# The last gate as seven block products, and the projection of p moved to the start of the kernel

## The chip, the cores and the metric

The kernel runs on one core of a Trainium2 chip. The metric is device time in microseconds (us). Engines are named as in the profile: PE is TensorE's matmul, PEld its weight load, DVE is VectorE, ACT is ScalarE, POOL is GpSimd, SP is SyncE, whose queue issues every DMA of this kernel.

## The reference

One layer of a hybrid encoder block on x (1024 tokens by 1024) and p (1024 tokens by 256), all in float32. The change touches the last two lines and nothing of the rest:

```python
h = rmsnorm(x, attn_norm[i]); proj = h @ w_in[i]          # q, k, v, conv_a, conv_g
...                                                       # attention, convolution, x = x + mix @ w_out[i]
h = rmsnorm(x, ffn_norm[i])
x = x + (jax.nn.silu(h @ w_gate[i]) * (h @ w_up[i])) @ w_down[i]
gate = jax.nn.sigmoid(rmsnorm(x, ple_norm[i]) @ w_ple_gate[i])   # (1024 x 1024) @ (1024 x 1024)
x = x + gate * (p[i] @ w_ple_proj[i])                            # (1024 x 256) @ (256 x 1024)
```

## The kernel before, in words

Every float32 product is made of three matmuls (`mm3`, L77): each operand is split into a high part h in a reduced float32 and a low part l = src - h (`split`, L69: ACT makes h, DVE or POOL makes l), and h·h, h·l and l·h are added in PSUM. A matmul has 128 x 128 stationary and 128 x 512 moving values.

The stages follow one another in the program text; a scheduler orders each engine's instructions by their place in the text and by what it expects to be ready, so that work of a later stage can stand among that of an earlier one. Each engine, and SP's queue, then works strictly in the order it was given.

- **Start** (L211 to L222): for each of 8 token tiles t, SP loads x, ACT squares it and DVE normalises it (`xn`, L115, after POOL's power of -0.5, `n_r`, L107), PE transposes it (L121), ACT and DVE split the result into `hT` and `lT`. Weights `wv` are loaded and split beside it, and the first four tiles of v (`pv`) are made from t = 4 on. Then come the convolution (its products `pg` and `pa` first), q, k, and attention.
- **Gate and up products, then the down product** of the feed-forward part, both already made by seven block products in place of eight (Winograd's form of Strassen's scheme: 2 x 2 blocks, sums of blocks multiplied, results combined). `dprod` (L814) is one of the seven down products: 11 steps of two DMAs into `dr`, a split and 12 matmuls. In the second of them the residual x is loaded back (`x1_load`, L798).
- **Last gate** (L878 to L929): for t = 0 to 7 the normed x is transposed and split into `h3`; two of the steps also load a half of p (`pin`), transpose it and split it (`ple_transpose`, L865). Then for two column halves and 8 token tiles: 24 matmuls into `pgt`, a sigmoid on ACT (`psg`), 6 matmuls into `pj` (p's projection), a multiply and an add of x on DVE (L927, L928), a DMA to the output. The very last tile does `pj` and what follows in two halves of 256 columns.

Of the kernel before, what the change touches and what calls it, by code (L numbers as in the profile page):

```python
# [17 lines left out]
P = 128  # L18
S = 1024
# [23 lines left out]
PLT = (0, 3)  # L43
# [9 lines left out]
def hybrid_block(ctx: ExitStack, tc: tile.TileContext, I, out):  # L53
# [760 lines left out]
    def dprod(name, banks, ai, bsrc, first):  # L814
        for p in range(NPR):
            r = cvy.tile([P, 2, 512], F32, name=f"dr{name}{p}", tag="y", bufs=4)
            dma(r[:, 0, :], ga_d[ai][p])
# [4 lines left out]
            l = dhl.tile([P, 2, 512], F32R, name=f"dl{name}{p}", tag="dhl", bufs=8)
            split(h, l, r)
            for q in range(4):
                a = slice(q * P, (q + 1) * P)
# [34 lines left out]
    w4 = es3.enter_context(sb_pool("w4", side="right"))  # L860
    pl = es3.enter_context(sb_pool("pl", side="right"))
    p_in = I["p"][0, 0].rearrange("(t p) c -> p t c", p=P)
    pT = []

    def ple_transpose(c):  # L865
        pin = rawp.tile([P, NT, P], F32, name=f"pin{c}", tag="raw", bufs=2)
        dma(pin, p_in[:, :, c * P:(c + 1) * P])
        h = cvy.tile([P, S], F32R, name=f"pTh{c}", tag="y", bufs=4)
        l = cvy.tile([P, S], F32R, name=f"pTl{c}", tag="y", bufs=4)
        for half in range(2):  # L870
            tp = tbank(f"ptp{c}{half}")
            for tt in range(4):
                nc.tensor.transpose(tp[:, tt, :], pin[:, 4 * half + tt, :], ident)
            hs = slice(half * 512, (half + 1) * 512)
            split(h[:, hs], l[:, hs], tp.rearrange("p a b -> p (a b)"))
        pT.append((h, l))

# [3 lines left out]
    H3 = [[op_pair(pool, f"h3{k}{i}", "act", 4) for i in range(2)] for k, pool in enumerate((map_, mcp))]  # L881

    def h3(w, half, k):
        return H3[k // 4][half][w][:, k % 4, :]

    wpg = I["w_ple_gate"][0].rearrange("(k p) c -> p k c", p=P)
    wpp = I["w_ple_proj"][0].rearrange("(k p) c -> p k c", p=P)
    gsets = [w_set(rawp, wpl, wpg, ch * 512, f"wpg{ch}", 2)
             for ch, wpl in enumerate(([(w8, 8)] * 4, [(w4, 4), (w4, 4), (w8, 8), (w8, 8)]))]
    for g in range(4):  # L890
        gsets[0][0](g)
    for t in range(NT):
        xn = sp3.tile([P, D], F32, name=f"n3_{t}_xn", tag="xin", bufs=2)
        xnorm(x1[:, t, :], gain3, xn, sp3, f"n3_{t}")
        for k in range(2):
            tsplit(xn[:, k * 512:(k + 1) * 512], H3[k][t // 4], t % 4, f"n3_{t}{k}")
        if t in PLT:
            ple_transpose(len(pT))
    for ch in range(2):
        cs = slice(ch * 512, (ch + 1) * 512)  # L900
        pload, wpj = w_set(rawp, [(pl, 2)], wpp, ch * 512, f"wpp{ch}", 2)
        pload(0)
        gload, ws = gsets[ch]
        if ch == 1:
            for g in range(4):
                gload(g)
        for t in range(NT):
            half, tt = t // 4, t % 4
            a = slice(tt * P, (tt + 1) * P)
            ps = mbank(f"pgt{ch}{t}")  # L910
            for k in range(KT):
                wh, wl = ws(k)
                mm3(ps, h3(0, half, k)[:, a], h3(1, half, k)[:, a], wh, wl, k == 0, k == KT - 1)
            sg = t5.tile([P, 512], F32, name=f"psg{ch}{t}", tag="t512", bufs=4)
            nc.scalar.activation(sg, ps, AF.Sigmoid)  # L915
            parts = 2 if ch * NT + t == 2 * NT - 1 else 1
            for i in range(parts):
                w = 512 // parts
                c0 = slice(i * w, (i + 1) * w)
                c1 = slice(ch * 512 + i * w, ch * 512 + (i + 1) * w)  # L920
                pj = mbank(f"pj{ch}{t}{i}")[:, 0:w]
                for k in range(2):
                    wh, wl = wpj(k)
                    mm3(pj, pT[k][0][:, t * P:(t + 1) * P], pT[k][1][:, t * P:(t + 1) * P], wh[:, c0], wl[:, c0],
                        k == 0, k == 1)
# [3 lines left out]
                dma(out[t * P:(t + 1) * P, c1], o)  # L929
# [43 lines left out]
```

## Time and profile before

| what | value |
|---|---|
| median of 3 runs | 1306.11 us (1303.47 to 1308.98) |
| the profiled execution: its own time | 1309.01 us |
| its span, first to last instruction | 1307.2 us |
| PE busy, share of the span | 1263.3 us, 97% |
| DVE, ACT, POOL busy | 68%, 43%, 29% |
| moved by DMA | 193.17 MB, mean 148 GB/s |
| granted TensorE clock, mean | 0.993 |

The durations used below come from that one execution, whose time is 2.9 us above the median. Matmuls are pipelined: what one costs is the distance between the starts of two, not the length in its row.

### The profile page before, as it was taken

Reading aid. Unit: us, or ns where it says so; the run is one execution under the profiler, and the core shown is the slowest. Engines: PE = TensorE matmul, PEld = TensorE weight load, DVE = VectorE, ACT = ScalarE, POOL = GpSimd, SP = SyncE. Lnnn points to the kernel's source line nnn. Section 1 sums busy time; section 2 is a strip of 40 time slices with the busy share of each in tenths; the row PEclk is TensorE's granted clock in tenths of the full one; section 3 lists DMA queues with packets and bytes.
Section 4 is the critical chain, followed back from the end, with each engine's and each line's share of the span. In section 5 each row is a group of like instructions: output and inputs, shape, how many; then the busy total and the mean of one; then the engine's idle time right before and its main releaser. Section 6 shows DMA issues by size and latency. Waiting matters only on the chain.

```text
span 1307.2 us, 16337 instructions
## 1 busy us (share of the span) xinstructions
PE 1263.3 (97%) x6015; PEld 1032.6 (79%) x6015; DVE 892.0 (68%) x1150; ACT 558.2 (43%) x818; POOL 377.4 (29%) x229
## 2 busy tenths in 40 slices
PE   6999999989989999889999999999999999999998
PEld 5888877858878888668888888888887788888887
DVE  6488999778868867966777666767655555566322
ACT  5465654556667654512322222222234443445110
POOL 4399987746665634710000000000000000000000
PEclk9999999999999999989999999999999999999999
DMA  8521323795463335344544544445439765641111
GB/s 277 171 65 33 119 75 105 174 241 122 114 167 109 106 105 193 114 161 153 169 161 161 169 146 161 145 153 164 168 139 383 235 193 192 195 159 65 49 57 41
DMA packets 156868, 193.17 MB, mean 148 GB/s; under 512 B 10919, under 2 KB 91317, under 8 KB 156788
## 3 DMA queue, kind: packets, MB, share of 16 engines
q1 hardware_dynamic: 156788, 192.13, 46.6%
q8 instruction: 47, 0.77, 0.2%
q14 instruction: 33, 0.27, 0.1%
HBM read 134.88 MB, written 57.21 MB: 147 GB/s over the span
## 4 chain that ended last, share of the span: by engine, by line
PE 79%; DVE 9%; DMA 6%; issue 2%; POOL 2%; ACT 1%; SPq 0%; DVEq 0%; POOLq 0%; ACTq 0%
PE Y L79 4%; PE Y L80 4%; PE Y L81 4%; PE Z L79 3%; PE Z L80 3%; PE Z L81 3%; PE X L81 3%; PE X L79 3%; PE X L80 3%; PE dY L79 2%; PE dY L80 2%; PE dY L81 2%; PE pgt L81 2%; PE pgt L80 2%; PE pgt L79 2%
## 5 line engine op out<-in xcount | busy, mean ns | idle before, releaser
L107 POOL TENSOR_TENSOR n_r<-n_ss,mhalf 128x1 f32<-128x1 f32 x24 | 15.0, 631 | 680.8 <-DVE n_ss L106 680.8
L75 DVE TENSOR_TENSOR dl<-dr,dh 128x1024 fp32r<-128x1024 f32 x77 | 94.1, 1224 | 73.8 <-ACT dh L72 71.1
L72 ACT CAST dh<-dr 128x1024 fp32r<-128x1024 f32 x77 | 80.6, 1049 | 105.5 <-PE dY L81 43.8
L316 POOL TENSOR_TENSOR z<-z,pr 128x1024 f32<-128x1024 f32 x45 | 115.8, 2575 | 3.1 <-ACT pr L315 0.8
L311 DVE SCALAR_TENSOR_TENSOR acc<-u,cw,acc 128x1024 f32<-128x1024 f32 x71 | 91.2, 1285 | 1.5
L530 ACT ACTIVATE e<-s,nm 128x1024 f32<-128x1024 f32 x64 | 71.6, 1119 | 37.0 <-DVE nm L527 30.4
L527 DVE TENSOR_REDUCE nm<-s 128x1 f32<-128x1024 f32 x64 | 77.4, 1219 | 10.0 <-PE s L523 4.9
L539 POOL TENSOR_TENSOR e<-e,e 128x1024 f32<-128x1024 f32 x32 | 77.7, 2429 | 2.4
L315 ACT ACTIVATE pr<-u,cw 128x1024 f32<-128x1024 f32 x45 | 51.0, 1149 | 36.4 <-POOL z L316 35.8
L522 PE MATMUL s<-ka,qa 128*128 128x512 f32 x128 | 57.1, 446 | 2.0 <-ACT e L530 1.9
L538 POOL TENSOR_SCALAR e<-e,cf 128x1024 f32<-128x1024 f32 x32 | 36.6, 1144 | 66.4 <-DVE cf L537 28.0
L927 DVE TENSOR_TENSOR o<-pj,psg 128x512 f32<-128x512 f32 (+1 forms) x17 | 11.2, 659 | 63.8 <-PE pj L81 55.5
L80 PE MATMUL dY<-dl,dh 128*128 128x512 f32 x132 | 51.4, 389 | 0.0
L81 PE MATMUL dY<-dh,dl 128*128 128x512 f32 x132 | 51.4, 389 | 0.0
L523 PE MATMUL s<-kb,qb 80*128 80x512 f32 x128 | 51.2, 400 | 0.0
L79 PE MATMUL dY<-dh 128*128 128x512 f32 x132 | 50.4, 391 | 0.0
L75 DVE TENSOR_TENSOR wtl<-wt,wth 128x512 fp32r<-128x512 f32 x64 | 43.2, 683 | 10.5 <-ACT wth L72 10.0
L72 ACT CAST wth<-wt 128x512 fp32r<-128x512 f32 x64 | 36.8, 587 | 20.0 <-PE wt L544 19.7
L915 ACT ACTIVATE psg<-pgt 128x512 f32<-128x512 f32 x16 | 9.6, 599 | 75.6 <-PE pgt L81 75.6
L755 DVE TENSOR_TENSOR aa<-Z,aa 128x512 f32<-128x512 f32 x22 | 15.2, 689 | 36.8 <-PE Z L81 36.8
L80 PE MATMUL av<-wtl,avh 128*128 128x256 f32 x128 | 39.0, 305 | 0.0
L79 PE MATMUL av<-wth,avh 128*128 128x256 f32 x128 | 37.9, 296 | 0.2 <-ACT wth L72 0.2
(355 smaller groups left out, 3979.9 us busy)
## 6 DMA issues: line engine op xcount, KB each, us to landing
dr<-ga_d SPq DMA_DIRECT2D x77, 256.0 KB, 2.7
wr<-in_w_gate SPq DMA_DIRECT2D x44, 256.0 KB, 3.0
wr<-in_w_up SPq DMA_DIRECT2D x44, 256.0 KB, 3.5
wd<-in_w_down SPq DMA_DIRECT2D x22, 512.0 KB, 3.6
wb_d<-wd SPq DMA_DIRECT2D x44, 256.0 KB, 2.0
ga_d<-h SPq DMA_DIRECT2D x44, 256.0 KB, 2.4
dr<-wb_d SPq DMA_DIRECT2D x44, 256.0 KB, 2.9
dr<-in_w_down SPq DMA_DIRECT2D x33, 256.0 KB, 5.3
```

The lines of the kernel that those rows point to most:

```text
L72: nc.scalar.copy(h, src)
L75: (eng_l or nc.vector).tensor_sub(l, src, f32(h))
L79: nc.tensor.matmul(ps, lh, rh, start=first, stop=False, skip_group_check=more)
L80: nc.tensor.matmul(ps, lh, rl, start=False, stop=False, skip_group_check=more)
L81: nc.tensor.matmul(ps, ll, rh, start=False, stop=last, skip_group_check=more)
L311: nc.vector.scalar_tensor_tensor(acc, u[:, k:k + S], cw[:, j, k:k + 1], acc, ALU.mult, ALU.add)
L316: nc.gpsimd.tensor_add(y2, y2, pr)
L522: nc.tensor.matmul(o, qa[:, m, ts_], ka[:, m, kc * 512:(kc + 1) * 512], start=True, stop=False)
L523: nc.tensor.matmul(o, qb[:, m, ts_], kb[:, m, kc * 512:(kc + 1) * 512], start=False, stop=not diag)
L527: nc.vector.tensor_reduce(nm, sp, AX.X, ALU.max, negate=True)
L530: nc.scalar.activation(e, sp, AF.Exp, bias=nm, accum_out=s)
L539: nc.gpsimd.tensor_add(es[0], es[0], es[1])
```

## The change: what it does

Three things, and the diff below is cut to them.

1. **p's projection is made at the start.** p comes already transposed as an input (`pT`), so that it isn't transposed on the chip. `pj_load` loads p and `w_ple_proj` in quarters, at first ahead of x, and splits them; `pj_tile` makes one of 16 tiles (128 x 512) with 6 matmuls, copies it out of PSUM (DVE and ACT by turns) and stores it to `pj_d` in device memory. Four tiles follow each of the first four norms of x.
2. **The last gate is made by seven products** of 512 x 512 blocks (`gprod`, 48 matmuls each: 4 token tiles, 4 steps, 3 parts). Sums of blocks of the normed x are built on DVE and POOL after the transposes (`fs1`, `f11`, `f12`, `f21`) and split afterwards by `comb_split`. Sums of blocks of `w_ple_gate` are made inside the down product (`gate_comb`): 4 times two loads of 512 KB, four subtractions on DVE, four stores of 256 KB to `tg_d`; `gprod` loads them again.
3. **Each output tile** now loads its projection (`pjl`), and goes through `finish`: sigmoid, multiply, add, store; 12 of the 16 have an add ahead of the sigmoid. The last tile is not halved any more.

```diff
+    def pj_load(nms, i):
+        raws = [rp1.tile([P, 2, 512], F32, name=f"{nm}{i}_raw", tag="raw", bufs=3) for nm in nms]
...
+        for k in range(2):
+            for nm, raw in zip(nms, raws):
+                h, l = pq[nm, i]
+                dma(raw[:, k, :], {"p": pT, "w": wpp}[nm][:, k, i * 512:(i + 1) * 512])
+                split(h[:, k, :], l[:, k, :], raw[:, k, :])
+
+    def pj_tile(i):
...
+        ps = mm_tile(f"pj{i}")
+        for k in range(2):
+            mm3(ps, ph[:, k, a], pl[:, k, a], wh[:, k, :], wl[:, k, :], k == 0, k == 1)
+        pj = nat.tile([P, CW], F32, name=f"pjs{i}", tag="nat", bufs=6)
+        if i % 2:
+            nc.scalar.copy(pj, ps)
+        else:
+            nc.vector.tensor_copy(pj, ps)
+        dma(pj_d[i], pj)
+
+    pj_load("pw", 0)
     for t in range(NT):
         xt = cvy.tile([P, D], F32, name=f"x{t}", tag="y", bufs=4)
         dma(xt, x[t * P:(t + 1) * P, :])
...
+        if t == 0:
+            pj_load("p", 1)
+        if t == 1:
+            pj_load("w", 1)
...
         norm_transpose(xt, gain1, t, hT, lT, p1m, f"n1_{t}", xn)
+        for i in range(4):
+            if t < 4:
+                pj_tile(4 * t + i)
...
+            if name == "62" and p in (1, 3, 5, 7):
+                gate_comb(p // 2)
...
+    def gate_comb(k):
+
+        d0 = rawp.tile([P, D], F32, name=f"wg{k}0", tag="raw", bufs=2)
+        d1 = rawp.tile([P, D], F32, name=f"wg{k}1", tag="raw", bufs=2)
+        for i, d in enumerate((d0, d1)):
+            dma(d, wpg[(4 * i + k) * P:(4 * i + k + 1) * P, :])
+        b11, b12, b21, b22 = d0[:, 0:512], d0[:, 512:D], d1[:, 0:512], d1[:, 512:D]
+        V.tensor_sub(b11, b12, b11)
...
+        for i, b in enumerate((b11, b22, b12, b21)):
+            dma(tg_d[i][k], b)
...
+            if t < 4:
+                h, l = A[("pa11", "pa12")[k]]
+                split(h[:, :, ts_], l[:, :, ts_], tp)
+                nc.scalar.copy((f11, f12)[k][:, :, ts_], tp)
+            elif k == 0:
+                nc.scalar.copy(f21[:, :, ts_], tp)
+            else:
+                V.tensor_add(fs1[:, :, ts_], tp, f21[:, :, ts_])
+                h, l = A["pa22"]
+                split(h[:, :, ts_], l[:, :, ts_], tp)
+        if t >= 4:
+            c11, c12, c21, cs1 = [f[:, :, ts_] for f in (f11, f12, f21, fs1)]
+            nc.gpsimd.tensor_sub(c21, c11, c21)
+            V.tensor_sub(c11, cs1, c11)
+            nc.gpsimd.tensor_sub(c12, c12, c11)
...
+        steps = [(g, q) for g in range(2) for q in q4]
+        if last:
+            steps = [(g, q) for q in q4 for g in range(2)]
+        for g, q in steps:
+            a = slice(q * P, (q + 1) * P)
+            for k in range(2):
+                mm3(banks[q], ah[:, 2 * g + k, a], al[:, 2 * g + k, a], ws[g][0][:, k, :], ws[g][1][:, k, :],
+                    first and g + k == 0, g + k == 2, not first)
...
-                mm3(ps, h3(0, half, k)[:, a], h3(1, half, k)[:, a], wh, wl, k == 0, k == KT - 1)
...
-                o = t5.tile([P, w], F32, name=f"o{ch}{t}{i}", tag="t512", bufs=4)
-                nc.vector.tensor_mul(o, pj, sg[:, c0])
-                nc.vector.tensor_add(o, o, x1[:, t, c1])
...
+        pj = pl.tile([P, 512], F32, name=f"pjl{ch}{t}", tag="pj", bufs=4)
+        dma(pj, pj_d[ch * NT + t])
+        nc.scalar.activation(o, src, AF.Sigmoid)
+        V.tensor_mul(o, pj, o)
+        V.tensor_add(o, o, x1[:, t, cs])
+        dma(out[t * P:(t + 1) * P, cs], o)
...
+    gprod("11", GX, "pa11", gblk(0, 0), True)
...
+    comb_split("ps1", fs1)
+    gprod("12", GX, "pa12", gblk(1, 0), False)
+    comb_split("ps2", f11)
+    for q in q4:
+        finish(otile(q, 0), GX[q], q, 0)
...
+    gprod("51", GZ, "ps1", gcmb(0), True)
...
+    gprod("44", GY, "pa22", gcmb(3), False, True)
+    for q in q4:
+        o = otile(4 + q, 0)
+        V.tensor_add(o, GY[q], e1[q // 2][:, q % 2, :])
+        finish(o, o, 4 + q, 0)
```

How the order moves at three places.

PE at its first instructions, before: it begins with the transposes of the first normed tile of x (`n1_0_tp`), then v's first tile.

```order
L121 MATMUL n1_0_tp0_150<-ident_70,xn0_143 128x128 x4
L121 MATMUL n1_0_tp1_157<-ident_70,xn0_143 128x128 x4
L79 MATMUL pv0_274<-wv0_h_139,hT00_125 128x512
L80 MATMUL pv0_274<-wv0_l_140,hT00_125 128x512
L81 MATMUL pv0_274<-wv0_h_139,lT00_129 128x512
```

PE with the change, where the same transposes now stand (rows 19 to 28 of its list, after four tiles of the projection, `pj0` to `pj3`; `p0`, `p1` and `w0` are halves of p and of its weight).

```order
L79 MATMUL pj1_211<-w0_l_148,p0_h_145 128x512
L80 MATMUL pj1_211<-w0_h_147,p0_l_146 128x512
L79 MATMUL pj2_221<-w0_l_148,p0_h_145 128x512
L80 MATMUL pj2_221<-w0_h_147,p0_l_146 128x512
L79 MATMUL pj3_231<-w0_l_148,p0_h_145 128x512
L80 MATMUL pj3_231<-w0_h_147,p0_l_146 128x512
L121 MATMUL n1_0_tp0_187<-ident_86,xn0_180 128x128 x4
L121 MATMUL n1_0_tp1_194<-ident_86,xn0_180 128x128 x4
L78 MATMUL pj4_279<-w0_h_147,p1_h_166 128x512
L79 MATMUL pj4_279<-w0_l_148,p1_h_166 128x512
```

24 matmuls of the projection stand ahead of the first transpose, and all 96 ahead of v's first matmul; from the convolution's first tile up to the last of the gate and up products, PE's order is the same but for some twenty rows in attention.

SP's queue at its start, with the change (from its third DMA on; two of the same kind stand ahead).

```order
L223 DMA p0_raw_143<-in_pT 128x512
L223 DMA w0_raw_144<-in_w_ple_proj 128x512
L243 DMA x0_161<-in_x 128x1024
L245 DMA ident_86<-in_c_ident 128x128
L246 DMA gain1_134<-in_attn_norm 128x1024
L223 DMA p1_raw_165<-in_pT 128x512 x2
L243 DMA x1_241<-in_x 128x1024
L127 DMA wv0_raw_174<-in_w_in 128x2x512
L243 DMA x2_319<-in_x 128x1024
L223 DMA w1_raw_243<-in_w_ple_proj 128x512 x2
```

Before, x's first tile was the first DMA and `wv0` the fourth; now four DMAs of 256 KB stand ahead of x.

DVE in the last gate with the change, at the end of product "12" (`gX`) and the start of "51" (`gZ`), whose operand is `ps1`; `ps2` is that of "62", after it.

```order
L949 TENSOR_TENSOR fs1_10495<-n3_71_10673,f21_10494 128x4x128
L1002 TENSOR_TENSOR o01_10841<-pjl01_10842,o01_10841 128x512
L1002 TENSOR_TENSOR o02_10848<-pjl02_10849,o02_10848 128x512
L1003 TENSOR_TENSOR o01_10841<-o01_10841,x2_8890 128x512
L74 TENSOR_TENSOR ps2l_10825<-f11_10492,ps2h_10824 128x4x128
L74 TENSOR_TENSOR pa22l_10491<-n3_71_10673,pa22h_10490 128x4x128
L1003 TENSOR_TENSOR o02_10848<-o02_10848,x2_8890 128x512
L955 TENSOR_TENSOR f11_10492<-fs1_10495,f11_10492 128x4x128
L74 TENSOR_TENSOR ps1l_10755<-fs1_10495,ps1h_10754 128x4x128
L74 TENSOR_TENSOR ps2l_10825<-f11_10492,ps2h_10824 128x4x128 x2
```

None of these stood there before. The first nine lead from the last transposed tile of x (`n3_71`) to the last quarter of `ps1l`, which product "51" multiplies, and one of the nine (`ps2l`) waits for product "12" to end, since `ps2` lies in the buffer of `pa12`.

## Rows read from the trace of the kernel before

**Rows 1.** The page: busy time of the engines, and the chain's shares by engine

```profile
PE 1263.3 (97%) x6015; PEld 1032.6 (79%) x6015; DVE 892.0 (68%) x1150; ACT 558.2 (43%) x818; POOL 377.4 (29%) x229
PE 79%; DVE 9%; DMA 6%; issue 2%; POOL 2%; ACT 1%; SPq 0%; DVEq 0%; POOLq 0%; ACTq 0%
```

**Rows 2.** Stretches of the span: busy us (and instructions) by engine

```profile
core 0: us, PE busy (x) PEld busy (x) DVE busy (x) ACT busy (x) POOL busy (x), PEclk, DMA share, GB/s
0.00:10.00 10.00, 1.41 (x7) 1.42 (x8) 2.10 (x4) 3.74 (x5) 1.10 (x12) 1.00 0.74 277
10.00:20.00 10.00, 7.36 (x29) 4.85 (x28) 9.01 (x10) 7.88 (x14) 3.44 (x3) 1.00 0.86 298
20.00:30.00 10.00, 10.00 (x44) 8.12 (x42) 8.68 (x9) 6.76 (x10) 6.46 (x5) 0.83 0.95 283
...
160.00:180.00 20.00, 18.64 (x84) 14.89 (x83) 19.93 (x17) 11.76 (x15) 19.55 (x9) 1.00 0.31 93
980.00:1000.00 20.00, 20.00 (x90) 16.54 (x89) 11.26 (x10) 8.52 (x10) 0.00 (x0) 1.00 1.06 395
1000.00:1010.00 10.00, 8.92 (x38) 6.77 (x37) 6.59 (x7) 5.31 (x7) 0.00 (x0) 1.00 1.04 355
...
1070.00:1080.00 10.00, 10.00 (x46) 8.29 (x45) 5.26 (x5) 3.40 (x4) 0.00 (x0) 1.00 0.77 243
...
1230.00:1240.00 10.00, 10.00 (x45) 8.21 (x44) 1.39 (x2) 1.20 (x2) 0.00 (x0) 1.00 0.07 26
```

**Rows 3.** Timeline of PE, start: start us, length us, instruction, idle before

```profile
8.59 1.97 PE L121 MATMUL n_tp<-ident,xn 128*128 128x128 f32 x8 [8.59 <-DVE xn L115]
...
19.67 0.66 PE L121 MATMUL n_tp<-ident,xn 128*128 128x128 f32 x4 [2.59 <-DVE lT L75]
...
43.23 0.39 PE L79 MATMUL pg<-hT,wg_h 128*128 128x512 f32 x1
```

**Rows 4.** Timeline of the end, PE and DVE

```profile
1289.22 0.39 PE L79 MATMUL pgt<-wpg_h,h301h 128*128 128x512 f32 x1
...
1296.18 0.39 PE L79 MATMUL pgt<-wpg_h,h301h 128*128 128x512 f32 x1
...
1303.04 0.28 PE L81 MATMUL pj<-wpp_h,pTl 128*128 128x256 f32 x1
...
1303.96 0.43 DVE L928 TENSOR_TENSOR o<-o,x 128x256 f32<-128x256 f32 x1
```

**Rows 5.** Tiles `pgt` and `pj`: instructions, ns min/median/max, first and last start

```profile
L79 PE MATMUL pgt<-wpg_h,h300h x32: 390/396/483, 1186.8 to 1270.4; 128*128 128x512 f32 x32
L79 PE MATMUL pj<-wpp_h,pTh x34: 278/397/399, 1192.4 to 1302.8; 128*128 128x512 f32 x30, 128*128 128x256 f32 x4
```

**Rows 6.** The chain in order of time, start of the kernel: a group of four transposes

```profile
33.23 0.44 PE n_tp L121 x4
```

**Rows 7.** Timeline of ACT, DVE and POOL, start

```profile
4.37 1.06 ACT L113 ACTIVATE xn<-x 128x1024 f32<-128x1024 f32 x1 [2.37 <-DMA x<-in_x]
15.62 3.40 DVE L115 SCALAR_TENSOR_TENSOR xn<-x,n_r,gain 128x1024 f32<-128x1024 f32 x1 [0.66 <-POOL n_r L107]
37.13 1.29 DVE L115 SCALAR_TENSOR_TENSOR xn<-x,n_r,gain 128x1024 f32<-128x1024 f32 x1
15.55 2.38 POOL L75 TENSOR_TENSOR wv_l<-wv_raw,wv_h 128x1024 fp32r<-128x1024 f32 x1
```

**Rows 8.** Waits from 960 to 1040 us: total us, times, longest

```profile
ACT dh L72 <- DMA dr<-in_w_down: 21.5, 16, 6.0
```

**Rows 9.** Timeline of DVE in the last gate, two instructions back to back

```profile
1203.47 0.68 DVE L75 TENSOR_TENSOR h301l<-n,h301h 128x512 fp32r<-128x512 f32 x1
1204.08 0.68 DVE L927 TENSOR_TENSOR o<-pj,psg 128x512 f32<-128x512 f32 x1
```

**Rows 10.** The page's groups: a split of 1024 columns on DVE (busy us, mean ns)

```profile
L75 DVE TENSOR_TENSOR dl<-dr,dh 128x1024 fp32r<-128x1024 f32 x77 | 94.1, 1224 | 73.8 <-ACT dh L72 71.1
```

**Rows 11.** Tile `n_xn`: a subtraction of 512 columns on POOL

```profile
L661 POOL TENSOR_TENSOR n_xn<-n_xn,n_xn x4: 1270/1295/1302, 511.3 to 534.7; 128x512 f32<-128x512 f32 x4
```

More of the change, by code (lines that the diff above doesn't have):

```diff
@@ L42 @@
 HNT = (0, 3)
-PLT = (0, 3)
 NVL = 2
@@ L97, in hybrid_block @@
     part_d = dram.tile([S, D], F32, name="part_d")
+    pj_d = [dram.tile([P, 512], F32, name=f"pj_d{i}") for i in range(2 * NT)]
     bias_d = dram.tile([(NH + 1) * NB, S], F32R, name="bias_d")
@@ L594, in hybrid_block @@
     ga_d = [[dram.tile([P, 512], F32, name=f"ga_d{i}_{p}") for p in range(NPR)] for i in range(7)]
+    tg_d = [[dram.tile([P, 512], F32, name=f"tg_d{i}_{k}") for k in range(4)] for i in range(4)]
     wb_d = [[dram.tile([P, 512], F32, name=f"wb_d{i}_{p}") for p in range(NPR)] for i in range(4)]
@@ L857, in hybrid_block, with pair, block @@
     es6.close()
-    w4 = es3.enter_context(sb_pool("w4", side="right"))
+    ap = es3.enter_context(sb_pool("ap", side="right"))
     pl = es3.enter_context(sb_pool("pl", side="right"))
[L862 to L876, printed above, removed]
     gain3 = sp3.tile([P, D], F32, name="gain3", tag="gain", bufs=1)
     dma(gain3, I["ple_norm"].to_broadcast([P, D]))
[L881 to L891, printed above, removed]
+    def pair(name, pool=None):
+        return op_pair(pool or map_, name, "act" if pool is None else "a22", 4 if pool is None else 2)
+    def block(name):
+        return mcp.tile([P, 4, 512], F32, name=name, tag="act", bufs=4)
+    A = {n: pair(n) for n in ("pa11", "pa12")}
+    A["pa22"] = pair("pa22", ap)
+    f11, f12, f21, fs1 = block("f11"), block("f12"), block("f21"), block("fs1")
     for t in range(NT):
@@ L894, in hybrid_block @@
         xnorm(x1[:, t, :], gain3, xn, sp3, f"n3_{t}")
+        ts_ = slice(t % 4 * P, (t % 4 + 1) * P)
         for k in range(2):
[L896 to L899, printed above, removed]
[L900 to L929 removed]
@@ new lines, in gcmb, with gprod @@
+    def gcmb(i):
+        return lambda g: [tg_d[i][2 * g + k] for k in range(2)]
+    def gprod(name, banks, a, bsrc, first, last=False):
+        ah, al = A[a]
+        ws = []
+        for g in range(2):
+            r = cvy.tile([P, 2, 512], F32, name=f"gr{name}{g}", tag="y", bufs=4)
+            src = bsrc(g)
+            if isinstance(src, list):
+                for k in range(2):
+                    dma(r[:, k, :], src[k])
+            else:
+                dma(r, src)
+            h = w8.tile([P, 2, 512], F32R, name=f"gh{name}{g}", tag="whl", bufs=8)
+            l = w8.tile([P, 2, 512], F32R, name=f"gl{name}{g}", tag="whl", bufs=8)
+            split(h, l, r)
+            ws.append((h, l))
+        steps = [(g, q) for g in range(2) for q in q4]
[3 more added lines that the diff above has]
+            a = slice(q * P, (q + 1) * P)
+            for k in range(2):
+                mm3(banks[q], ah[:, 2 * g + k, a], al[:, 2 * g + k, a], ws[g][0][:, k, :], ws[g][1][:, k, :],
+                    first and g + k == 0, g + k == 2, not first)
@@ new lines, in finish, with otile @@
+    def finish(o, src, t, ch):
+        cs = slice(ch * 512, (ch + 1) * 512)
+        pj = pl.tile([P, 512], F32, name=f"pjl{ch}{t}", tag="pj", bufs=4)
[4 more added lines that the diff above has]
+        dma(out[t * P:(t + 1) * P, cs], o)
+    def otile(t, ch):
+        return t5.tile([P, 512], F32, name=f"o{ch}{t}", tag="t512", bufs=4)
+    GX = [bank(f"gX{q}", n=q) for q in q4]
@@ new lines, in hybrid_block @@
+    gprod("11", GX, "pa11", gblk(0, 0), True)
+    e1 = [rawp.tile([P, 2, 512], F32, name=f"ge{i}", tag="raw", bufs=2) for i in range(2)]
+    for q in q4:
+        nc.scalar.copy(e1[q // 2][:, q % 2, :], GX[q])
+    comb_split("ps1", fs1)
+    gprod("12", GX, "pa12", gblk(1, 0), False)
+    comb_split("ps2", f11)
+    for q in q4:
+        finish(otile(q, 0), GX[q], q, 0)
+    GZ = [bank(f"gZ{q}", n=4 + q) for q in q4]
+    gprod("51", GZ, "ps1", gcmb(0), True)
+    z5 = block("gz5")
+    for q in q4:
+        V.tensor_add(z5[:, q, :], GZ[q], e1[q // 2][:, q % 2, :])
@@ new lines, in hybrid_block @@
+    comb_split("ps4", f12)
+    GY = [bank(f"gY{q}", n=q) for q in q4]
+    gprod("62", GY, "ps2", gcmb(1), True)
+    aa = block("gaa")
+    for q in q4:
+        V.tensor_add(aa[:, q, :], GY[q], e1[q // 2][:, q % 2, :])
+    comb_split("ps3", f21)
+    gprod("34", GZ, "ps4", gblk(1, 1), False)
+    for q in q4:
+        o = otile(q, 1)
+        V.tensor_add(o, GZ[q], aa[:, q, :])
+        finish(o, o, q, 1)
+    gprod("73", GY, "ps3", gcmb(2), False)
+    for q in q4:
+        o = otile(4 + q, 1)
+        V.tensor_add(o, GY[q], z5[:, q, :])
+        finish(o, o, 4 + q, 1)
```

36 lines of the change are left out of this document (32 added, 4 removed).

## Prediction

> **What bounds the kernel now.** I read the page first: PE is busy for 97% of the span and makes 79% of the chain that ended last [rows 1]. So I took the stretches next, to see where PE is not full. In the last gate it is full to the last tenth, with DVE at 1.4 us of 10 and DMA at 7% [rows 2]: there, each matmul taken away ends the kernel one matmul earlier, as long as the rest follows. At the start PE is not full: it does nothing until the first tile of x is loaded and normed, at 8.59 us, and waits another 2.59 us at 19.67 [rows 3]. Around 980 to 1010 us, in the first down products, DMA is (share 1.04 to 1.06) and PE loses about 1 us in 10 [rows 2]. From 160 to 180 us DVE is full and PE loses 1.4 us [rows 2]; this work keeps its order, so it moves with the start and costs neither more nor less.
>
> The price of a matmul is read from the end, where two tiles' first matmuls stand 6.96 us apart with 30 matmuls between: 0.232 us each [rows 4].
>
> **The change, part by part.**
>
> *The gate's products.* Before: 12 groups of `pgt` matmuls, 32 in each, make 384 [rows 5]. Seven products of 48 are 336. 48 x 0.232 = **-11.1 us**, all on the path, since PE has no gap there.
>
> *The projection leaves the end.* Three groups of 30 whole and 4 half matmuls are worth 96 whole ones [rows 5]: 96 x 0.232 = **-22.3 us**.
>
> *The transposes of p* were four groups of four at 0.44 us [rows 6]: **-1.8 us**. The 16 groups of x stay.
>
> *The last tile's tail.* Before, DVE ended at 1303.96 + 0.43 = 1304.4 us, 1.2 us after the last matmul's end near 1303.2, because the tile was halved [rows 4]. Now add, sigmoid, multiply and add follow the last matmul, each 512 wide and 0.6 to 0.7 us [rows 9]: about 2.8 us, and a store of 256 KB in place of 128. **+1.8 us**; its ends are 1.4 (no gaps) and 2.5.
>
> *The projection at the start.* 96 matmuls more are 22.3 us of PE. What covers them: x's first tile, the first DMA of the queue, was there at 4.37 us [rows 7], and the first quarters of p and of its weight are together as large, so they can be there at about 4.4; with ACT's half of a split (0.6 us) PE can start at 5.0, not 8.59: -3.6. The wait of 2.59 us can be filled: -2.6. After that wait the granted clock was 0.83 on average from 20 to 30 us [rows 2]: about 3.4 us of these ran at the lower level, 1.2 in place of 2.4 GHz, and lost 1.7; without the wait ahead of it I take back 1.5: -1.5. That leaves 14.6 us. Against it: DVE was busy 9.0 and 8.7 us of 10 from 10 to 30 us [rows 2], and gets 8 splits and 8 copies of 512 columns, about 0.61 us each back to back [rows 9], 10 us in all; in its order they stand between the norms, and some of PE's 96 matmuls will wait for a copy to free a bank. I put 2 us on that: **+16.6 us**. The ends: 13 us where DVE never holds PE, and 24 us where nothing is covered (22.3) and x, behind 1 MB of p and w, comes 2 us later. The loads themselves (2 MB) and the stores (4 MB) ride at 280 to 300 GB/s already moving [rows 2]; the weights of v and of the convolution, queued behind the stores on SP, are now needed some 16 us later too, so I cost that at nothing; without that cover each 256 KB store is about 0.9 us of queue.
>
> *The blocks of the gate's weight in the down product.* 4 MB are loaded and 4 MB stored, while 3 MB (gate weights and p) are not loaded there any more: 5 MB more. In 980 to 1000 us DMA moved 395 GB/s and was full [rows 2], and ACT waited 21.5 us in 16 times for the down product's operands [rows 8]. In SP's order as much new traffic stands before the end of that jam as the old weights and p had there, some 2.5 MB each; the rest falls later, where DMA has a quarter free (0.77 busy from 1070 to 1080) [rows 2]. DVE's 16 subtractions, 0.61 us each, are 10 us beside 7 x 11 x 12 = 924 matmuls, over 200 us of PE. I take **+1 us**; the ends are 0 and 12.8 (5 MB at 395 GB/s, nothing hidden).
>
> *New waits in the gate.* DVE now has, from the last down product on: 83 instructions of 512 columns at 0.61 us [rows 9], 10 weight splits at 1.22 [rows 10] and four norms at 1.3 [rows 7]: 68 us, beside 336 x 0.232 + 11 groups of transposes x 0.44 = 83 us of PE. The tightest place is the last quarter of `ps1`: the last tile of x is transposed about 24 us after the down product ends, product "12" ends at about 27, and `ps1l` is the ninth DVE instruction after these transposes: about 31 us, while PE wants that quarter 32 matmuls into "51", at about 34.5. I take **+1 us**; ends 0 and 20 (below).
>
> Row: POOL subtracts 512 columns in 1.3 us [rows 11], and DVE's norm of 1.29 us took 3.40 while POOL split a weight beside it [rows 7]. The Trainium skill says the same of the cause (GPSIMD Engine Reference, Specifications): GpSimd's SBUF interfaces are shared with VectorE, with contention for DVE instructions that have two SBUF inputs. It speaks against this change: the 8 new POOL subtractions, 10.3 us, would be added to DVE's 68 us in the gate, 78 of 83; the sum would still be as above but for the slack of `ps1`, and about 2 us higher.
>
> **Sum:** -11.1 - 22.3 - 1.8 + 1.8 + 16.6 + 1 + 1 = **-14.8 us**. The profiled execution (1309.0) would be 1294.2; the median shown is 2.9 lower, so 1306.1 - 14.8 = **1291.3 us**.
>
> **The rivals.**
>
> *The start is covered better.* DVE keeps up and PE starts dense: +13 at the start, nothing in the down product and the gate: 1306.1 - 35.2 + 1.8 + 13 = 1285.7. For it: 8.6 and 2.6 us of idle PE. Against it: DVE's 9 of 10.
>
> *The start isn't covered.* The loads of p push x back, the copies of the projection push the norms back on DVE, PE waits between them and falls to the lower clock after each wait: 24 us at the start, 1299.7 with 2 us elsewhere. For it: the one wait of 2.59 us before, and DVE. Against it: PE has 24 matmuls ahead of the first norm, six groups of them to bridge the others.
>
> *The jam in the down product grows.* A store of `tg_d` waits on SP for a DVE subtraction, which waits for a load in the jam, and the operands queue behind: half to all of 12.8 us: 1298 to 1303. For it: the queue is strict and full at 1.05. Against it: four operand tiles (`dr`) and four split ones (`dh`, `dl`) can be ahead of PE.
>
> *The gate becomes DVE's, slower than before.* A split of a sum can only start when the product that read its buffer has ended. If the splits of a product run after the end of the one before it, not beside it, then five products each wait for four splits and a part of the weights on DVE, 4 x 0.61 + 2 x 1.22 = 4.9 us, 24 us in all, and each wait would let the clock fall: 1291.3 + 24 = 1315. It decides when a product needs what was freed only one product ago. Against it: `ps1` is read by "51", one product after "11" freed its buffer, and so on: each has a whole product (11 us) for 5 us of DVE. For it: DVE's 68 to 78 us of 83, in strict order.
>
> *It doesn't do what it says.* If p's loads landed so late that PE still began with x, the start would cost its full 22.3, 1297; the order puts 24 matmuls of the projection first, and x's landing at 4.4 us speaks against loads so late; its chance is part of the uncovered start's.
>
> **How the numbers follow.** Forecast (1287 to 1296) 0.58; better covered start (1285 to 1287) 0.12; uncovered start, with the projection that changes nothing there, 0.15 (1296 to 1301); jam 0.09 (1298 to 1303); DVE-bound gate 0.06 (1310 and over). About 0.5% (6.5 us) is what a measurement of this kernel can tell from no change; below 1299.6 lie the first two, 0.12 of the third and 0.04 of the jam: 0.86 faster. The rest of these two, 0.08, is the same, and the last case, 0.06, slower. The range of 8 in 10 runs from 1284 to 1300: from just under the better start to the end of the uncovered one.
>
> **What would show it.** In the profile after: first matmul of PE at about 5 us and the first of the convolution's products (`pg`), at 43.23 before [rows 3], at about 58 to 62, all transposes of x done; from the last down matmul to the last gate matmul about 84 us, where it was 118; the last matmul followed by 2.8 us of ACT and DVE; in 980 to 1020 us no PE wait over 2 us; DVE near 8 of 10 in the gate with PE still full. I am wrong if `pg` starts after 66 us, if PE shows waits on `ps` splits or on `tg_d` loads of several us, or if the gate's matmuls stand further apart than 0.232 us.

## The result and the profile after

The changed kernel takes **1290.52 us** (median of 4 runs, 1288.63 to 1292.45), the kernel before 1306.21 in the same rounds (4 runs, 1303.47 to 1308.98): a ratio of 0.9871, 95% interval 0.9848 to 0.9893. Timed again later, it took 1292.07 us, ratio 0.9882 (0.9865 to 0.9899). The forecast was 1291.3, faster.

The profiled execution took 1289.18 us (span 1287.4), a second one had a span of 1291.9; the one of before had 1307.2. The table cuts these spans at matmuls that all kernels have: the first `pk` (the projection of k, behind the convolution's products), the first transpose of `tt`, the last `X`, the first and last of the down product, the last matmul of the program. From the last `X` to the first down matmul it is 22.3 us in all of them.

| stretch, us | before | changed | changed, again |
|---|---|---|---|
| start to the first `pk` | 156.2 | 170.4 | 170.2 |
| `pk` to `tt` (projections of q and k, attention) | 362.9 | 360.4 | 365.2 |
| `tt` to the last `X` (gate and up products) | 429.3 | 431.7 | 431.6 |
| down product | 214.2 | 213.4 | 213.4 |
| last down matmul to the last matmul (gate) | 118.1 | 82.9 | 82.9 |
| last matmul's start to the end of the span | 4.2 | 6.3 | 6.3 |

So the pair of profiles shows -19.8, and the second one -15.3: the two executions of one program differ by 4.8 in the attention alone. The stretches that the change touches agree within 0.3 us.

The page, as in [rows 1]:

```profile
PE 1249.3 (97%) x5945; PEld 1021.1 (79%) x5945; DVE 937.5 (73%) x1220; ACT 583.0 (45%) x862; POOL 394.4 (31%) x237
PE 81%; DVE 7%; DMA 6%; issue 2%; POOL 2%; ACT 1%; SPq 1%; DVEq 0%; POOLq 0%; ACTq 0%
```

PE has 14 us less, DVE 45 more. The stretches of the changed kernel, columns as in [rows 2], with the whole gate as the last:

```profile
core 0: us, PE busy (x) PEld busy (x) DVE busy (x) ACT busy (x) POOL busy (x), PEclk, DMA share, GB/s
10.00:20.00 10.00, 10.00 (x54) 8.23 (x53) 8.90 (x14) 8.77 (x16) 1.23 (x2) 1.00 1.03 402
20.00:30.00 10.00, 10.00 (x53) 8.18 (x53) 10.00 (x16) 8.27 (x17) 2.84 (x5) 1.00 1.05 408
...
1230.00:1240.00 10.00, 10.00 (x45) 8.11 (x44) 10.00 (x15) 5.74 (x9) 5.31 (x2) 1.00 0.57 178
...
1198.20:1281.50 83.30, 83.27 (x382) 67.80 (x380) 72.89 (x100) 42.39 (x68) 19.46 (x12) 1.00 0.43 139
```

At the start PE is full from 10 us on, with the granted clock at 1.00, where it was 0.83 from 20 to 30 us, and DMA moves 400 GB/s. In the gate PE is as full as before, and DVE, at 1.4 of 10 before, has 72.9 us of 83.3 and is busy throughout from 1230 to 1240. The start on PE, as in [rows 3]:

```profile
4.83 2.07 PE L78 MATMUL pj<-w_h,p_h 128*128 128x512 f32 x4 [4.83 <-ACT w_h L71]
12.18 1.04 PE L121 MATMUL n_tp<-ident,xn 128*128 128x128 f32 x8
...
33.12 1.25 PE L121 MATMUL n_tp<-ident,xn 128*128 128x128 f32 x8 [0.49 <-DVE lT L74]
...
59.44 0.39 PE L78 MATMUL pg<-hT,wg_h 128*128 128x512 f32 x1
```

The first transposes of x come 3.6 us later than before, behind 24 matmuls of the projection, and up to `pk` the only wait after 4.83 is 0.49 us. The end, as in [rows 4] (DVE and ACT behind the last matmul):

```profile
1281.07 0.40 PE L80 MATMUL gY<-gh,pa22l 128*128 128x512 f32 x1
1281.51 0.69 DVE L1044 TENSOR_TENSOR o<-gY,ge 128x512 f32<-128x512 f32 x1
...
1282.23 0.63 ACT L1001 ACTIVATE o<-o 128x512 f32<-128x512 f32 x1 [2.17 <-DVE o L1044]
1282.89 0.69 DVE L1002 TENSOR_TENSOR o<-pjl,o 128x512 f32<-128x512 f32 x1 [0.69 <-ACT o L1001]
1283.62 0.69 DVE L1003 TENSOR_TENSOR o<-o,x 128x512 f32<-128x512 f32 x1
```

Add, sigmoid, multiply, add: 2.8 us in a chain.

### The profile page after: what moved, and what is told of

It reads as the page before. It is cut to its first block, busy times and chain, and to the rows that moved or that the text cites. A ratio compares the mean times of both kernels' runs of the same rounds, so it can differ in the third digit from the quotient of the medians.

```text
span 1287.4 us, 16537 instructions
## 1 busy us (share of the span) xinstructions
PE 1249.3 (97%) x5945; PEld 1021.1 (79%) x5945; DVE 937.5 (73%) x1220; ACT 583.0 (45%) x862; POOL 394.4 (31%) x237
## 4 chain that ended last, share of the span: by engine, by line
PE 81%; DVE 7%; DMA 6%; issue 2%; POOL 2%; ACT 1%; SPq 1%; DVEq 0%; POOLq 0%; ACTq 0%
PE Y L78 5%; PE Y L79 5%; PE Y L80 5%; PE Z L79 3%; PE Z L78 3%; PE Z L80 3%; PE X L80 3%; PE X L78 3%; PE X L79 3%; PE dY L78 2%; PE dY L79 2%; PE dY L80 2%; PE s L562 2%; DVE acc L351 2%; PE s L563 2%
## 5 line engine op out<-in xcount | busy, mean ns | idle before, releaser
L107 POOL TENSOR_TENSOR n_r<-n_ss,mhalf 128x1 f32<-128x1 f32 x24 | 14.7, 617 | 670.1 <-DVE n_ss L106 661.6
L80 PE MATMUL X<-B11h,a11l 128*128 128x512 f32 x88 | 33.5, 401 | 6.5 <-DVE a11l L74 6.5
L584 PE MATMUL wt<-ident,e 128*128 128x128 f32 x256 | 37.5, 273 | 0.3 <-DVE wtl L74 0.2
```

What stands on the lines that cost most here:

```text
L80: nc.tensor.matmul(ps, ll, rh, start=False, stop=last, skip_group_check=more)
```

## The experiments

All ratios are to the kernel before in the same rounds.

**0. The changed kernel again** (`changed_again`).

> The changed kernel as it is, timed in the same rounds as the three below. Theory: as in its first runs, 1290.5, ratio 0.987. Its profile shows which stages move from one execution to the next: the start (`pk` at 170.4), the down product (213.4 us from its first to its last matmul) and the gate (82.9 us from the last down matmul to the last one) within 0.5 us, the attention and the first product behind it by 1 to 3 us.

Measured: as told above. The touched stretches repeat within 0.3 us, which makes them the finer measure below; the attention moves by more than was said.

**1. The projection moved alone** (`proj_moved_alone`). The kernel before, with the start of the change and this in its gate:

```diff
-                pj = mbank(f"pj{ch}{t}{i}")[:, 0:w]
-                for k in range(2):
-                    ...
-                nc.vector.tensor_mul(o, pj, sg[:, c0])
+                nc.vector.tensor_mul(o, pjl[:, c0], sg[:, c0])
```

> The kernel before with p's projection alone moved to the start; the gate keeps its 384 matmuls, its last tile is halved as before. Theory (idle time of PE at the start pays for part of it): the end loses 96 x 0.232 = 22.3 us of matmuls and 1.8 of transposes, the start gains the 14.3 us by which the first matmul of `pk` stands later in the changed kernel, so 9.8 us less than before, about 1296.5 (ratio 0.9925), with `pk` first near 170.5. Rival (the start isn't covered, the whole gain is the gate's): 22.3 to 24 at the start, ratio 0.998 to 1.000.

Measured: 1302.45, ratio 0.9955 (0.9939 to 0.9970). By stretches: first `pk` 170.7 (+14.5), gate 93.6 (-24.5), both as the theory has it; but +1.1 behind the last matmul (the sigmoid used to run beside the projection's matmuls, and now stands in the tail) and +3.8 from `tt` to the last `X`, which the edit doesn't touch. The theory of the start holds; the sum of 9.8 was too good by these two.

**2. No projection** (`no_projection`). `pj_load` and `pj_tile` and their calls are taken out of the changed kernel, and in `finish` a block of x stands in for the projection, so that the output leaves it out:

```diff
-        dma(pj, pj_d[ch * NT + t])
+        dma(pj, x[t * P:(t + 1) * P, cs])
```

> The changed kernel without any of the projection: p and its weight are not loaded, the 96 matmuls, their copies and stores are not made, and the last multiply takes a block of x of the same size in place of the projection. Theory: the start goes back to that of the kernel before (first matmul near 8.6 us, first of `pk` near 156), so about 14 us less than the changed kernel: 1276.5, ratio 0.977. Rival 1, the projection costs its full price or more there: 22 to 24 us less, 1267. Rival 2, it is hidden whole: no difference, 1290.5.

Measured: 1275.61, ratio 0.9752 (0.9724 to 0.9779); first `pk` at 155.7. The whole projection costs 14.7 us at the start, neither its full 22.3 nor nothing.

**3. The projection behind the norms** (`projection_after_norms`). In the changed kernel, the calls in the loop over x are taken out, and behind the loop stands

```diff
+    pj_load("pw", 0)
+    pj_load("p", 1)
+    pj_load("w", 1)
+    for i in range(2 * NT):
+        pj_tile(i)
     es0.close()
```

> The changed kernel with the loads, matmuls, copies and stores of the projection issued behind the loop of the norms and v's products, in place of among them. Theory: the saving at the start is idle time that the projection's matmuls fill, so here PE begins with x again near 8.6 us, the 96 matmuls cost 22.3 us in full, and the kernel takes about 8 us more than the changed one: 1298.5, ratio 0.994. Rival: the place doesn't matter, 1290.5, ratio 0.988.

Measured: 1303.18, ratio 0.9969 (0.9952 to 0.9986): 12 us slower than the changed kernel, first `pk` at 185.2, +29.0 to before and not +22.3. PE's waits up to 185 us:

```profile
PE n_tp L121 <- DVE xn L115: 9.1, 1, 9.1
PE n_tp L121 <- DVE lT L74: 2.6, 1, 2.6
PE pj L78 <- ACT pjs L235: 2.2, 1, 2.2
PE pa L78 <- ACT wa_h L71: 1.7, 1, 1.7
PE pa L80 <- POOL wa_l L74: 0.4, 1, 0.4
```

The first two are those of the kernel before, unfilled. The next three, 4.3 us, are new. ACT's order makes them:

```profile
67.27 1.04 ACT L71 CAST wg_h<-wg_raw 128x1024 fp32r<-128x1024 f32 x1 [5.40 <-DMA wg_raw<-in_w_in]
68.22 1.07 ACT L235 COPY pjs<-pj 128x512 f32<-128x512 f32 x2
71.79 0.59 ACT L235 COPY pjs<-pj 128x512 f32<-128x512 f32 x1 [2.51 <-issue]
72.28 1.05 ACT L71 CAST wa_h<-wa_raw 128x1024 fp32r<-128x1024 f32 x1
```

The copies `pjs`, which free PE's banks, stand behind a split of the convolution's weights that waits 5.40 us for its load, and the split `wa_h` stands behind the last copy. SP issued that load at 62.41, when POOL had freed its buffer, not when a store let it through. The granted clock is also low a second time, 0.91 on average from 60 to 80 us, which is 1.8 us more. The place of the 96 matmuls decides their price.

**4. No sums of weight blocks** (`no_block_sums`). `gate_comb` and its call are left out, and the four `gcmb(i)` become `gblk(...)`: four products take raw blocks of the weight in place of sums.

> The changed kernel without the sums of the gate's weight blocks in the down product: they are not loaded, summed or stored (8 MB of traffic and 16 subtractions on DVE less), and the four products that want sums take raw blocks. Theory: this traffic rides beside matmuls; the down product had a wait of 1.0 us with it and 1.7 before, so within 1.5 us of the changed kernel, 1289 to 1291, ratio 0.987. Rival (the jam): half to all of 12.8 us less, 1278 to 1284.

Measured: 1290.05, ratio 0.9859 (0.9830 to 0.9888); down product 212.0 us, where the kernels with the sums have 212.7 to 213.8. They cost 0.7 to 1.8 us there; no jam.

**5. POOL's subtractions on DVE** (`pool_subs_on_dve`).

```diff
-            nc.gpsimd.tensor_sub(c21, c11, c21)
+            V.tensor_sub(c21, c11, c21)
             V.tensor_sub(c11, cs1, c11)
-            nc.gpsimd.tensor_sub(c12, c12, c11)
+            V.tensor_sub(c12, c12, c11)
```

> The changed kernel with the eight subtractions of POOL in the gate made by DVE. In the changed kernel six of DVE's instructions of 512 columns that run beside one of them take 1.0 to 1.8 us in place of 0.61, about 5.8 us more in all. Theory (the two engines hold each other up): these 5.8 us go and 8 x 0.61 = 4.9 come, so DVE is as full as before, the last split of `ps1` ends about 35 to 36 us after the down product, and the time stays within 1 us, 1290.5. Rival (what lengthens them is something else): DVE has 4.9 us more ahead of the last split of `ps1`, which had 0.8 us to spare; PE waits about 4 us in the product 51: 1294.5.

Measured: 1290.37, ratio 0.9871 (0.9854 to 0.9887); the gate 82.9 us, no wait of PE in it, and the last split of `ps1` ends 36.0 us after the down product in both. The subtractions in the changed kernel (tile `f`: ns min/median/max):

```profile
L949 DVE TENSOR_TENSOR fs<-n,f x4: 678/682/694, 1209.5 to 1227.1; 128x512 f32<-128x512 f32 x4
L954 POOL TENSOR_TENSOR f<-f,f x4: 1296/1488/1748, 1210.3 to 1228.3; 128x512 f32<-128x512 f32 x4
L955 DVE TENSOR_TENSOR f<-fs,f x4: 675/1196/1815, 1212.1 to 1233.0; 128x512 f32<-128x512 f32 x4
L956 POOL TENSOR_TENSOR f<-f,f x4: 1293/2240/5233, 1214.0 to 1233.7; 128x512 f32<-128x512 f32 x4
```

and with the edit:

```profile
L954 DVE TENSOR_TENSOR f<-f,f x4: 682/686/694, 1209.3 to 1230.8; 128x512 f32<-128x512 f32 x4
L955 DVE TENSOR_TENSOR f<-fs,f x4: 681/684/685, 1211.7 to 1234.5; 128x512 f32<-128x512 f32 x4
L956 DVE TENSOR_TENSOR f<-f,f x4: 683/687/693, 1214.2 to 1235.2; 128x512 f32<-128x512 f32 x4
```

With both inputs in SBUF, an instruction on either engine is lengthened by one on the other, DVE's from 0.68 to 1.8 us, POOL's from 1.3 to 5.2; alone on DVE all are 0.69 at most. Eight subtractions handed to POOL freed no time on DVE: in the gate's 83.3 us it is busy for 72.9 us in the changed kernel and for 72.3 with the edit. `fs<-n,f`, which reads `n` from PSUM, was never lengthened.

**6. More work on DVE in the gate** (`dve_plus_8`).

```diff
-                V.tensor_add(fs1[:, :, ts_], tp, f21[:, :, ts_])
+                for _ in range(3):
+                    V.tensor_add(fs1[:, :, ts_], tp, f21[:, :, ts_])
```

> The changed kernel with eight additions of 512 columns more on DVE in the gate (each of the four sums of the lower row's transposes is made three times, with the same result). Theory (DVE is the nearest limit there, the last split of `ps1` ends 0.8 us before PE wants it): 8 x 0.61 = 4.9 us more ahead of it, so PE waits 3 to 4 us in the product 51 and the kernel takes 3 to 4 us more: 1294, ratio 0.990. Rival (by the prediction's sum, 68 us of DVE beside 83 of PE, there is room): 1290.5, no wait of PE over 1 us.

Measured: 1294.94, ratio 0.9907 (0.9892 to 0.9922); the gate 86.6 us, +3.7. PE's waits there:

```profile
PE gY L80 <- DVE ps2l L74: 2.5, 2, 2.1
PE gY L79 <- DVE gl L74: 0.3, 1, 0.3
```

The size is the theory's; the place is one product later, since the planner (the scheduler that orders each engine's instructions) put matmuls of the product 62 ahead of those of 51 that would have waited.

**7. All copies on DVE** (`copies_on_dve`): in `pj_tile`, `nc.vector.tensor_copy(pj, ps)` for every tile.

> The changed kernel with all 16 copies of the projection's results out of their banks on DVE, in place of 8 on DVE and 8 on ACT. Theory (DVE, full from 20 to 30 us, is about to hold PE at the start, as the prediction's 2 us for it say): 8 x 0.61 = 4.9 us more on it, `pk` 2 to 5 us later than 170.4, time 1293 to 1295. Rival (there is room, since PE has matmuls of the projection and of v to go on with): `pk` within 0.5 us of 170.4, 1290.5.

Measured: first `pk` at 172.9, +2.5, as the theory has it, yet 1289.31 us, ratio 0.9859 (0.9843 to 0.9875), no slower. The stretch from `tt` to the last `X` was 429.1, not 431.7. This, and the 3.8 us of run 1, led to that stretch. DVE there, in the changed kernel (second pair of hidden blocks):

```profile
578.08 1.23 DVE L752 TENSOR_TENSOR s<-wr,wr 128x1024 f32<-128x1024 f32 x1 [6.14 <-DMA wr<-in_w_up]
...
581.67 0.69 DVE L786 TENSOR_TENSOR g<-X,g 128x512 f32<-128x512 f32 x1
585.75 1.22 DVE L761 TENSOR_TENSOR s<-wr,s 128x1024 f32<-128x1024 f32 x1 [3.40 <-DMA wr<-in_w_up]
586.90 1.22 DVE L74 TENSOR_TENSOR a11l<-wr,a11h 128x1024 fp32r<-128x1024 f32 x1
588.09 0.69 DVE L818 TENSOR_TENSOR wd<-wd 128x512 f32<-128x512 f32 x1
588.70 0.68 DVE L792 TENSOR_TENSOR bb<-Y,e 128x512 f32<-128x512 f32 x1
```

Both idle times are for loads. At 585.75 it is that of `a12`, for the sum `s4` (L761), and behind it stands `a11l`, for which PE waits 6.5 us (8.7 in the second profile); two rows on, `bb` (it combines this pair's products and frees PE's banks) stands behind `wd` (block sums of the down weights, for the next stage). In the kernels of before and of runs 2 and 7 the planner has it the other way at both places (`a11l`, `s4`, `bb`, `wd`); PE waits 4.2, 1.7 and 2.1 us for `a11l`. There it also waits for `bb`, 1.5, 3.1 and 2.4 us, which it doesn't in the changed kernel.

**8. `s4` off DVE's queue** (`s4_on_pool`).

```diff
-        V.tensor_sub(s4, a12, s2)
+        (nc.gpsimd if p == 1 else V).tensor_sub(s4, a12, s2)
```

> The changed kernel with one subtraction moved: `s4` of the second pair of hidden blocks (`s4 = a12 - s2`), which stands ahead of the split `a11l` on DVE in the changed kernel and behind it in the kernel before, is made by POOL. Theory: DVE's queue is held there by the load of `a12`, with `a11l` (its data there 10 us earlier) behind it, and PE waits for `a11l`, 6.5 to 8.7 us in the changed kernel's executions, 4.2 in the kernel before; without it the wait falls to 4 us or less, the stretch from the first transpose of `tt` to the last product of X from 431.6 us to about 429, and the time by 2 to 3 us, ratio 0.985 to 0.986. Rival (the loads are what is late, whichever instruction is first): the stretch stays at 431.6.

Measured: 1292.90, ratio 0.9879 (0.9858 to 0.9900), stretch 432.7. The theory fell:

```profile
PE Y L78 <- DVE bb L792: 4.6, 1, 4.6
PE X L80 <- DVE a11l L74: 1.8, 1, 1.8
```

Of 6.5 us for `a11l` 1.8 are left, but `wd`, still ahead of `bb`, now stands for its own load, 5.2 us, and PE waits for `bb`. The wait moved on by one instruction, because loads are late for both.

**9. Three edits together** (`s4_pool_subs_halves`): runs 8 and 5, and the last tile in halves:

```diff
+        for i in range(2):
+            c = slice(i * 256, (i + 1) * 256)
+            V.tensor_add(o[:, c], GY[q][:, c], e1[1][:, 1, c])
+            nc.scalar.activation(o[:, c], o[:, c], AF.Sigmoid)
+        for i in range(2):
+            c = slice(i * 256, (i + 1) * 256)
+            V.tensor_mul(o[:, c], pj[:, c], o[:, c])
+            V.tensor_add(o[:, c], o[:, c], x1[:, NT - 1, c])
+            dma(out[(NT - 1) * P:, c], o[:, c])
```

> The changed kernel with three edits together: `s4` of the second pair on POOL, POOL's eight subtractions of the gate on DVE, and the last output tile's sum, sigmoid, multiply, add and store in two halves of 256 columns. Theory: 2 to 3 us from the first, nothing from the second, 0.3 to 0.5 from the third (six instructions of 256 columns at about 0.37 us on DVE, the sigmoid of the first half beside them, and a last store of 128 KB): 1287.5 to 1289, ratio 0.9850. Rival: as the changed kernel, 0.988.

Measured: 1290.22, ratio 0.9866 (0.9845 to 0.9887): no gain that the timing shows. The tail is 5.7 us, 0.6 less; the stretch, 431.9, is unchanged as in run 8.

**10. The first pair's splits on DVE** (`first_pair_on_dve`).

```diff
-            split(h, l, src, None, nc.gpsimd if p == 0 else None)
+            split(h, l, src)
```

> The changed kernel with the splits of the first pair of hidden blocks on DVE in place of POOL. In the changed kernel DVE's four subtractions `wd` of that pair, beside POOL's splits, take 2.25 to 2.77 us in place of 0.61, 8 us more in all, and the loads of the next pair wait on SP behind their stores. Theory (the two engines hold each other up, and DVE pays more than it would for the work itself): seven splits of 1.22 us come on DVE, 8.5, and about 8 go, so the loads are no later and the stretch from `tt` to the last X changes by less than 2 us. Rival (POOL's share is free): 8 us later in that stretch.

Measured: **1284.24**, ratio 0.9812 (0.9791 to 0.9833), faster than the changed kernel; the stretch 427.5, better than either side had it, and 4 us shorter where the theory allowed 2. POOL and DVE in the changed kernel's timeline, where the stores of `wd` wait for these subtractions on SP, with loads of the next pair behind them:

```profile
561.74 2.85 POOL L74 TENSOR_TENSOR s1l<-s,s1h 128x1024 fp32r<-128x1024 f32 x1
...
562.36 2.77 DVE L819 TENSOR_TENSOR wd<-wd,wd 128x512 f32<-128x512 f32 x1
...
564.54 2.85 POOL L74 TENSOR_TENSOR s3l<-s,s3h 128x1024 fp32r<-128x1024 f32 x1
...
565.16 2.77 DVE L820 TENSOR_TENSOR wd<-wd,wd 128x512 f32<-128x512 f32 x1
```

DVE with the edit:

```profile
563.10 1.22 DVE L74 TENSOR_TENSOR s3l<-s,s3h 128x1024 fp32r<-128x1024 f32 x1
564.23 0.68 DVE L819 TENSOR_TENSOR wd<-wd,wd 128x512 f32<-128x512 f32 x1
...
565.43 0.68 DVE L820 TENSOR_TENSOR wd<-wd,wd 128x512 f32<-128x512 f32 x1
...
582.48 1.22 DVE L74 TENSOR_TENSOR a11l<-wr,a11h 128x1024 fp32r<-128x1024 f32 x1
583.61 1.21 DVE L761 TENSOR_TENSOR s<-wr,s 128x1024 f32<-128x1024 f32 x1
```

DVE does a split (1.22) and a subtraction (0.68) in less than the 2.77 us that the subtraction alone took beside POOL.

But the edit changed a second thing: the planner's order on DVE is that of the kernel before again (`a11l` ahead of `s4`, as shown, and `bb` ahead of `wd`), and `s4` no longer waits for its load. SP issued the last load of that pair at 582.20 us in the changed kernel, after 3.8 us of waiting for DVE's third sum (L759), and with the edit at 575.83:

```profile
582.20 0.51 SPq L737 DMA_DIRECT2D wr<-in_w_up  x1
```

```profile
575.83 0.58 SPq L737 DMA_DIRECT2D wr<-in_w_up  x1
```

PE waits 3.0 us for `a11l` in place of 6.5. How much of the gain comes from POOL's splits as such, and how much from the order, isn't told apart: beside the kernels with the old order (429.1 to 430.7) the stretch is 1.6 to 3.2 us shorter.

**11. Run 10 and the halves together** (`first_pair_halves`).

> The changed kernel with the first pair's splits on DVE and the last output tile in two halves. Theory: the stretch from `tt` to the last X near 427.5 us as with the first edit alone, 4 less than the changed kernel's 431.6, and 0.6 us less behind the last matmul (5.7 to the span's end, 6.3 in the changed kernel): 4.7 us less, 1286 to 1287, ratio 0.983 to 0.984. The first edit's own run was 7 us faster than the changed kernel's median; if these 7 hold again, 3 us come from a place that the stretch doesn't show (attention, 187.9 us there, 187 to 193 in the other runs), and the theory of the stretch is short by them.

Measured: **1282.67**, ratio 0.9819 (0.9797 to 0.9840), the stretch 422.7 and the tail 5.7. It beats both kernels, 0.982 beside 0.987 to 0.988 for the changed one; from run 10 it can't be told apart. The stretch is 4.1 us shorter than the changed kernel's (431.6) in run 10 and 8.9 here, where the theory had 4. Both kernels have the same order there, but PE waits 3.0 us for `a11l` in run 10 and not at all here; two single profiles don't show what the edit is worth on average.

## Why the prediction was right

**The gate's products, the projection and p's transposes out of the end:** -35.2 in the forecast (11.1 + 22.3 + 1.8), 118.1 to 82.9 = -35.2 measured. PE stays full, so each matmul taken away counted.

**The start:** forecast +16.6, measured +14.2 (`pk`) and 14.7 (run 2). The three credits came in: first matmul at 4.83 (5.0 said), one wait of 0.49 in place of 2.59, clock 1.00 in place of 0.83. `pg` at 59.44 lies in the 58 to 62 said; it moved by 16.2, 2.0 more than `pk`, since 20 of x's 64 transposes stood behind it before and none do now. The term that failed is "2 us on that", for PE's waits on DVE's copies: they were 0 to 0.5. Run 7 gives the room: 4.9 us more on DVE cost 2.5, so about half of such a load was still free. Run 3 shows what the cover is worth: 29.0 without it. The weights of v and of the convolution behind the stores on SP were put at nothing, and no wait of PE up to `pk` is for them.

**The down product:** forecast +1, measured -0.8. The sums themselves are +0.7 to +1.8 (run 4), so the term's size was right for what comes. Without the sums the stretch is 2.2 us shorter than before (212.0 and 214.2): what leaves it (the gate's old weights, p and its weight) gave back about that, which the prediction had set off only in the jam.

**New waits in the gate:** forecast +1, measured 0, but by less room than I said. The last split of `ps1` was to be ready at about 31 us and wanted at 34.5. It ended at 36.0:

```profile
1233.56 0.68 DVE L74 TENSOR_TENSOR ps1l<-fs,ps1h 128x512 fp32r<-128x512 f32 x1
...
1234.09 0.39 PE L80 MATMUL gZ<-gh,ps1l 128*128 128x512 f32 x1
1234.32 0.39 PE L78 MATMUL gY<-gh,ps2h 128*128 128x512 f32 x1
...
1235.01 0.40 PE L80 MATMUL gZ<-gh,ps1l 128*128 128x512 f32 x1
```

The planner had put three matmuls of `gY` (product 62) ahead of the first that reads this quarter, so it was 0.8 us early. Run 6 shows that DVE is the next limit: 4.9 us more cost 3.7. The rival "the gate becomes DVE's" was wrong, but with 4 to 5 us more work there DVE begins to hold PE.

**The tail:** forecast +1.8, measured +2.1, in its ends.

**DVE beside POOL.** The trace shows it at 72.9 us, between the 68 without and the 78 with all of POOL's time added, and lengthened on both sides. The Trainium skill (SBUF — State Buffer, "SBUF: two separate sides") says that DVE and GpSimd take one pair of ports in turn, for a whole instruction, where DVE has both inputs in SBUF. The runs agree: the subtraction that starts at 562.36 ends at 565.13, 0.54 us after POOL's split beside it, takes 2.77 us where it takes 0.68 alone (run 10), and an instruction that reads PSUM isn't lengthened (run 5). The 2 us that the prediction named for this effect did not come in the gate, where the lengthening used up room and not time. At 560 us it may cost the changed kernel time; run 10 gains 4 us or more there, but with the order changed too.

**What the sum missed:** +2.4 from `tt` to the last `X`, a stretch that the change doesn't touch. The planner orders the whole program anew, and exchanged two pairs on DVE there. The three executions with the order of before have 429.1 to 430.7 us, the seven with the new order 431.5 to 433.1 (without runs 8 to 11, which edit the place). That the order is the cause is likely from this, and not shown: moving `s4` alone gave nothing, and the whole order was not put back by itself. PE's waits and its clock both take part: over the 90 us from the first `tt` PE is busy for 79.2 us with 371 instructions before, for 78.6 and 76.2 with 360 in the two executions of the changed kernel, and the granted clock is 0.96 before, 0.92 and 0.94 after. Runs 10 and 11, where POOL's splits are gone and DVE's order is that of before, are the shortest. By stretches without the attention the change is -17.3 (14.2 - 0.8 + 2.4 - 35.2 + 2.1), where the forecast had -14.8: 2.4 too much at the start, 1.8 in the down product, 1 in the gate, 0.3 too little in the tail, and the 2.4 not seen. The two measured ratios, 0.9871 and 0.9882, are -16.9 and -15.4 us. The mechanism held term by term, but that the total came within 1 us of the median measured is luck in part: 5.2 us of cost that did not come stand against 2.7 that were not seen, and the attention moves by 4.8 from one execution to the next.

## What to carry to other kernels

Price a moved block of matmuls by what the engine does in the new place, unit by unit: here the same 96 cost 22.3 us at the end, 14.2 to 14.7 among the loads and norms, and 29 behind them. Before work is handed from VectorE to GpSimd, see whether the instructions on both have two inputs in SBUF; if so, the time may come back as longer instructions on both, as it did in run 5. Where a planner orders the program, compare the stretches that the change doesn't touch as well.

## What was not expected of the hardware

Two executions of the changed kernel differ by 4.8 us in the attention, with the same work. From 285 to 310 us, first execution and second:

```profile
285.00:310.00 25.00, 23.51 (x118) 16.98 (x117) 20.33 (x33) 15.07 (x24) 14.22 (x9) 0.93 0.92 233
```

```profile
285.00:310.00 25.00, 23.77 (x100) 16.80 (x98) 18.96 (x31) 14.01 (x23) 12.13 (x7) 0.77 0.83 218
```

PE is busy for the same 23.5 to 23.8 us, but the granted clock is 0.93 in one and 0.77 in the other, and 118 instructions are done in place of 100. At 1.2 in place of 2.4 GHz, a mean of 0.77 is 11.5 us at the lower level, 0.93 is 3.5: 8 us more at half speed are 4 us lost. This stretch (`pk` to `tt`) takes 359.0 to 365.2 us over the profiles of all kernels here; between the two executions of the changed kernel it is all of the difference, 4.5 us of span.
